# Cutting the first load of a row-normalising kernel into four row transfers

## The chip, the cores and the metric

The kernel runs on one core of one Trainium2 chip. The metric is the device time of one execution in microseconds (us). Most executions agree within 0.3%.

## The reference

```python
def setup_inputs():
    batch, dim = 1024, 4096
    return {"x": np.random.randn(batch, dim).astype(np.float32),
            "axis": -1, "eps": np.float32(1e-12)}

def reference(x, axis, eps):
    norm = np.sqrt(np.sum(x ** 2, axis=axis, keepdims=True) + eps)
    return (x / norm).astype(np.float32)
```

Each of 1024 rows of 4096 numbers is divided by its length. 16.78 MB are read and 16.78 MB are written.

## The kernel before

The input is cut into two tiles. A tile gives each of the 128 partitions R = 4 consecutive rows, 64 KB, so it holds 8.389 MB. Both loads are issued at the very start by SyncE, both stores later on the same queue.

```python
    R = 4
    ...
    x_t = x.rearrange("(p t r) d -> t p (r d)", t=n_tiles, r=R)
    out_t = out_flat.rearrange("(p t r) d -> t p (r d)", t=n_tiles, r=R)
    io = ctx.enter_context(tc.tile_pool(name="io", bufs=n_tiles))
    ...
    for i in range(n_tiles):
        g = RowGroups(nc, io, stats, scratch, D, R, eps_t)
        load = nc.sync.dma_start(out=g.flat(), in_=x_t[i])
        to_front(nc, load.ins)      # moves the load ahead of the opening barrier
        groups.append(g)

    for i, g in enumerate(groups):
        g.square_dve(R - 1)         # VectorE: sum of squares of row 3
        g.square_act(0)             # ScalarE: sum of squares of row 0
        g.norm(0)                   # square root (ScalarE), reciprocal (VectorE)
        g.scale(0)                  # VectorE
        g.square_act(1)
        g.norm(1)
        g.norm(R - 1)
        g.scale(1)
        g.scale(R - 1)
        g.square_act(2)
        g.norm(2)
        if i < n_tiles - 1:
            g.scale_by_both(2)      # 7/8 of the row on ScalarE, 1/8 on VectorE
        else:
            g.scale(2)
        store = nc.sync.dma_start(out=out_t[i], in_=g.flat())
```

The rows are scaled in place. Each tile has a buffer of its own, so no buffer is waited for.

Of the kernel before, what the change touches and what calls it, by code (L numbers as in the profile page):

```python
# [82 lines left out]
def to_front(nc, load):  # L83






    def move(program):  # L90
        blocks = program.main_func.blocks
        entry = blocks[0].instructions
        if any(i.name == load.name for i in entry):
            return
        body = next(
            b.instructions
            for b in blocks
            if any(i.name == load.name for i in b.instructions)
        )
        at = next(n for n, i in enumerate(body) if i.name == load.name)  # L100
        assert not body[at].sync_info.on_wait
        before = next(
            n
            for n, i in enumerate(entry)
            if i.engine == mybir.EngineType.SP and isinstance(i, mybir.InstDrain)
        )
        entry.insert(before, body.pop(at))

    nc.at_finalize(move)
# [72 lines left out]
@with_exitstack  # L182
def kernel(
    ctx: ExitStack,
    tc: tile.TileContext,
    x: bass.AP,
    axis: bass.AP,
    eps: bass.AP,
    out: bass.AP,
):  # L190
    nc = tc.nc
    P = nc.NUM_PARTITIONS

    assert isinstance(axis, int) and axis in (-1, len(x.shape) - 1)
    eps = float(eps)

    x = x.flatten_outer_dims()
    out_flat = out.flatten_outer_dims()
    N, D = x.shape
    R = 4  # L200
    assert N % (P * R) == 0
    n_tiles = N // (P * R)
# [4 lines that stand above are left out]
    scratch_pool = ctx.enter_context(tc.tile_pool(name="scratch", bufs=1))  # L207
    stats = ctx.enter_context(tc.tile_pool(name="stats", bufs=n_tiles))

    eps_t = scratch_pool.tile([P, 1], F32)  # L210
    nc.vector.memset(eps_t, eps)  # L211
    sq_act = scratch_pool.tile([P, D], F32)
    sq_dve = scratch_pool.tile([P, D], F32)
    scratch = {"act": sq_act, "dve": sq_dve}

    groups = []
    for i in range(n_tiles):
        g = RowGroups(nc, io, stats, scratch, D, R, eps_t)
        load = nc.sync.dma_start(out=g.flat(), in_=x_t[i])  # L219
        to_front(nc, load.ins)  # L220
        groups.append(g)

    for i, g in enumerate(groups):
        g.square_dve(R - 1)
        g.square_act(0)
        g.norm(0)
        g.scale(0)
# [8 lines that stand above are left out]
            g.scale_by_both(2)  # L236
# [3 lines that stand above are left out]
    gpsimd_waits_for_last_store(nc, store.ins)  # L240
# [35 lines left out]
```

## Time and profile before

| what | value |
|---|---|
| time, before the prediction | 81.85 us, median of 3 (81.83 to 81.91) |
| span of the profiled execution | 79.9 us |
| load 0 landed | 21.81 us |
| load 1 landed | 41.14 us |
| store 0, store 1 issued | 38.71 us, 56.50 us |
| VectorE, ScalarE busy | 26.7 us, 29.7 us |

A landing is read here from the start of the first instruction that waits for it. The profile has two more things: the page's share of the 16 DMA engines' time, and the packet records in the trace, which give start, duration and size of each packet that an engine moved. `prof` does not print them; they were read from the trace file. A record does not name its engine, so the records are taken in order of start, 16 at a time, one for each engine. In the steady state a packet of 64 KB has a record of 2.418 us, and the records of one engine follow each other every 2.414 us.

### The profile page before, as it was taken

What the parts mean: (1) busy time and instruction counts of PE and PEld (TensorE: products, weight loads), DVE (VectorE), ACT (ScalarE), POOL (GpSimd) and SP (SyncE); (2) the same over time, 40 slices, a digit from 0 to 9 for tenths busy, and PEclk for the clock granted to TensorE, in tenths of its full rate; (3) what the DMA queues carried; (4) which work ended last, traced back from release to release, by engine and by line L of the source; (5) the groups of instructions that cost most, each with busy time, mean ns of one, the idle gap of its engine ahead of it and who ended that gap; (6) DMA issues with size and microseconds to landing.
All of it is one profiled execution on the core that took longest, in us unless ns stands there. A gap on an engine that the chain in (4) does not pass through costs nothing.

```text
span 79.9 us, 93 instructions
## 1 busy us (share of the span) xinstructions
DVE 26.7 (33%) x21; ACT 29.7 (37%) x23; POOL 0.2 (0%) x4
## 2 busy tenths in 40 slices
DVE  0000000000099599960049995999200000000000
ACT  3200000000099999989349999950000000000000
POOL 1000000000000000000000000000000000000000
DMA  9099996599996699993899991999974999965990
GB/s 492 33 525 525 525 525 295 230 525 525 525 525 262 262 525 525 525 525 164 361 525 525 525 459 66 525 525 525 525 328 197 525 525 525 525 295 230 525 525 0
DMA packets 576, 33.55 MB, mean 420 GB/s; under 512 B 64, under 2 KB 64, under 8 KB 64
## 3 DMA queue, kind: packets, MB, share of 16 engines
q1 hardware_dynamic: 576, 33.55, 97.6%
HBM read 16.78 MB, written 16.78 MB: 420 GB/s over the span
## 4 chain that ended last, share of the span: by engine, by line
DMA 51%; ACT 10%; DVE 9%; SPq 0%; issue 0%
DMA xt<-in_x_dram 51%; ACT sq_act L33 9%; DVE xt L64 9%; ACT rstd L53 1%; SPq L219 0%; DVE rstd L59 0%
## 5 line engine op out<-in xcount | busy, mean ns | idle before, releaser
L33 ACT ACTIVATE sq_act<-xt 128x4096 f32<-128x4096 f32 x6 | 21.7, 3609 | 21.7 <-DMA xt<-in_x_dram 21.7
L42 DVE SCALAR_TENSOR_TENSOR sq_dve<-xt 128x4096 f32<-128x4096 f32 x2 | 8.8, 4424 | 25.7 <-DMA xt<-in_x_dram 25.7
L64 DVE TENSOR_SCALAR xt<-xt,rstd 128x4096 f32<-128x4096 f32 x7 | 16.5, 2353 | 0.2
L72 ACT ACTIVATE xt<-xt,rstd 128x3584 f32<-128x3584 f32 x1 | 3.3, 3282 | 0.2 <-DVE rstd L59 0.2
L53 ACT ACTIVATE rstd<-ssq,eps_t 128x1 f32<-128x1 f32 x8 | 2.1, 289 | 0.1
L59 DVE RECIPROCAL rstd<-rstd 128x1 f32<-128x1 f32 x8 | 1.3, 159 | 2.4 <-ACT rstd L53 2.4
L33 ACT ACT_TABLE_LOAD x1 | 1.3, 1283 | 1.3 <-PEq L257 1.3
L53 ACT ACT_TABLE_LOAD x1 | 1.3, 1283 | 0.0
L33 ACT ACTIVATION_READ_ACCUMULATOR sq_act<-xt 128x1 f32 x6 | 1.1, 186 | 0.0
L211 DVE MEMSET eps_t<- 128x1 f32 x1 | 0.1, 59 | 1.3 <-PEq L257 1.3
L78 DVE TENSOR_SCALAR xt<-xt,rstd 128x512 f32<-128x512 f32 x1 | 0.5, 486 | 0.0
L42 DVE DVE_READ_ACCUMULATOR sq_dve<-xt 128x1 f32 x2 | 0.2, 82 | 0.0
L257 POOL MEMSET const-bfloat16-1.0<- 128x1 bf16 x1 | 0.1, 103 | 0.0
L257 POOL MEMSET const-uint8-127<- 128x1 uint8 x1 | 0.1, 102 | 0.0
L257 POOL MEMSET const-float32-0.0<- 128x1 f32 x1 | 0.1, 100 | 0.2 <-issue 0.2
L257 POOL MEMSET const-float32-1.0<- 128x1 f32 x1 | 0.1, 99 | 0.0
## 6 DMA issues: line engine op xcount, KB each, us to landing
xt<-in_x_dram SPq DMA_DIRECT2D x2, 31.2
out_dram<-xt SPq DMA_DIRECT2D x2, 22.5
```

What stands on the lines that cost most here:

```text
L33: self.nc.scalar.activation(out=sq_a, in_=self.x[:, r], func=ACT_F.Square, accum_out=self.ssq[:, r : r + 1],)
L42: self.nc.vector.scalar_tensor_tensor(out=sq_v, in0=self.x[:, r], scalar=1.0, in1=self.x[:, r], op0=ALU.mult, op1=ALU.mult, accum_out=self ...
L53: self.nc.scalar.activation(out=self.rstd[:, r : r + n], in_=self.ssq[:, r : r + n], func=ACT_F.Sqrt, bias=self.eps_t,)
L59: self.nc.vector.reciprocal(out=self.rstd[:, r : r + n], in_=self.rstd[:, r : r + n])
L64: self.nc.vector.tensor_scalar_mul(out=self.x[:, r], in0=self.x[:, r], scalar1=self.rstd[:, r : r + 1])
L72: self.nc.scalar.activation(out=self.x[:, r, :cut], in_=self.x[:, r, :cut], func=ACT_F.Copy, scale=rstd,)
L78: self.nc.vector.tensor_scalar_mul(out=self.x[:, r, cut:], in0=self.x[:, r, cut:], scalar1=rstd)
L211: nc.vector.memset(eps_t, eps)
L257: nc = _bacc.Bacc("TRN2", target_bir_lowering=False, num_devices=1)
```

## The change

The intent: with tile 0 in four pieces, row 0 can be squared when a quarter of the tile is there, instead of both compute engines waiting until 21.8 us for all of it.

```diff
     for i in range(n_tiles):
         g = RowGroups(nc, io, stats, scratch, D, R, eps_t)
-        load = nc.sync.dma_start(out=g.flat(), in_=x_t[i])
-        to_front(nc, load.ins)
+        pieces = R if i == 0 else 1
+        for j in range(pieces):
+            part = slice(j * R * D // pieces, (j + 1) * R * D // pieces)
+            load = nc.sync.dma_start(out=g.flat()[:, part], in_=x_t[i][:, part])
+            to_front(nc, load.ins)
         groups.append(g)
```

## The prediction

> **What bounds the kernel now.** I began with the page of the profiled execution, because it says at once whether an engine or the transfers carry the span. These are lines of its parts 1, 2, 3 and 4:
>
> ```profile
> DVE 26.7 (33%) x21; ACT 29.7 (37%) x23; POOL 0.2 (0%) x4
> ...
> DMA packets 576, 33.55 MB, mean 420 GB/s; under 512 B 64, under 2 KB 64, under 8 KB 64
> ...
> q1 hardware_dynamic: 576, 33.55, 97.6%
> ...
> DMA 51%; ACT 10%; DVE 9%; SPq 0%; issue 0%
> ```
>
> The third line decides. The one queue moves 33.55 MB (16.78 MB of input, as much of output), and its packets fill 97.6% of the time of all 16 DMA engines. VectorE and ScalarE are busy for a third. The chain in the last line (51% transfer, then ScalarE and VectorE) is a trap: it adds up to 70%, because it stops at the issue of the last store, and that store is not on it. A chain of compute in it does not mean that compute is the bound.
>
> So I read the timeline next, for when the transfers are issued and when the compute engines are let go. Columns: start, duration, engine, line, operation, and idle time before it:
>
> ```profile
> 0.00 0.86 SPq L219 DMA_DIRECT2D xt<-in_x_dram  x2
> ...
> 21.81 3.62 ACT L33 ACTIVATE sq_act<-xt 128x4096 f32<-128x4096 f32 x1 [19.26 <-DMA xt<-in_x_dram]
> ...
> 38.71 18.13 SPq L239 DMA_DIRECT2D out_dram<-xt  x2
> 41.14 4.42 DVE L42 SCALAR_TENSOR_TENSOR sq_dve<-xt 128x4096 f32<-128x4096 f32 x1 [5.25 <-DMA xt<-in_x_dram]
> ...
> 54.12 2.35 DVE L64 TENSOR_SCALAR xt<-xt,rstd 128x4096 f32<-128x4096 f32 x1
> 56.50 0.34 SPq L239 DMA_DIRECT2D out_dram<-xt  x1
> ```
>
> Both loads are issued by 0.86 us. Load 0 has landed at 21.81 us and load 1 at 41.14 us, so one tile of 8.389 MB takes 41.14 - 21.81 = 19.33 us, 434 GB/s, and the start-up before the first tile is 21.81 - 19.33 = 2.48 us. Store 0 is issued at 38.71 us, 2.4 us before load 1 ends; store 1 at 56.50 us, while store 0 should end at about 41.14 + 19.33 = 60.5 us, so 4.0 us early. Neither store comes too late, hence the queue should never run dry. Two stretches, cut at those landings, confirm it (second column the length; last two the DMA share and GB/s):
>
> ```profile
> 21.80:41.14 19.34, 12.45 (x10) 16.55 (x12) 0.00 (x0) 1.00 1.00 434
> 41.14:60.00 18.86, 14.23 (x10) 11.87 (x10) 0.00 (x0) 1.00 0.99 431
> ```
>
> The DMA share is 1.00 during load 1 and 0.99 while store 0 runs. (Shares near the edges of a stretch are rounded by whole 64 KB packets.) My model of the kernel is then 2.48 us of start-up plus 4 x 19.33 = 77.32 us, 79.80 us, against a span of 79.9 us. The measured 81.85 us is 1.95 us more than the span; I carry that over unchanged.
>
> **What the Trainium skill says.** First, "Perfetto Trace Analysis", section DMA Optimizations: splitting transfers may let work start sooner and finish sooner "if DMA engines are generally idle". Here they are not: 97.6% busy. Second, "DMA: Bandwidth & Descriptors", Where 436 GB/s comes from: 16 ports x 32 B x 850 MHz = 435.2 GB/s. The trace agrees: 434 GB/s is 99.7% of it, so there is no faster rate for a different cutting to find. Third, the same page, Queues, rings and completion order: each DMA engine consumes the descriptors of a ring in order. The trace agrees where it can be seen: load 1, issued 0.4 us after load 0, lands one whole tile time after it. Fourth, the same page, Latency and other measured facts: copies of 16 KiB rows with a row pitch of 512 KiB in HBM ran at only 207 GB/s. The pitch here is 8 rows x 16 KiB = 128 KiB, before and after, and the trace shows 434 GB/s at it with 64 KiB runs; no trace yet shows it with 16 KiB runs.
>
> **The change part by part.** It removes one load of 128 x 64 KB, and adds four of 128 x 16 KB to the same bytes, on the same queue, still in front of load 1.
>
> *Issue.* Two loads took 0.86 us to issue, 0.43 each. Five take about 2.15 us, and load 1 is issued at about 1.7 us instead of 0.43. Load 0 keeps the queue full until about 21.8 us, so this is hidden. The first piece still covers 128 partitions, so all 16 engines start as before.
>
> *Packets.* A load has 128 packets of 64 KB, 8 per engine; now load 0 has 512 of 16 KB, 32 per engine, 24 more. The fixed cost of a packet is an estimate from the rate above: 64 KB takes 19.33 / 8 = 2.416 us on an engine, and at the skill's 27.2 B/ns (435.2 / 16) it would take 2.409; about 7 ns are left. So 24 x 7 = 0.17 us. The tile also gets three more completion writes per engine; their records in the trace last 9 ns each, 0.03 us. These 0.20 us lie on the saturated queue and so on the path that sets the end. It is probably an upper figure, as part of the 7 ns is the completion write of the tile; I take 0.15.
>
> *Compute of tile 0.* The pieces should land at about 2.48 + 4.87 n: 7.4, 12.2, 17.1 and 22.0 us. ScalarE squares rows 0, 1 and 2 as they land (3.6 us each); the order of the compiled program has VectorE now scale rows 0 and 1 and its eighth of row 2 before it squares row 3. After the last piece come VectorE's square 4.42, read-out 0.08, square root and reciprocal with their hand-overs about 0.5, and a scale of 2.35: 7.4 us. ScalarE's share of row 2 is done at about 17.1 + 3.6 + 0.2 + 0.3 + 0.4 + 3.3 = 24.9, sooner. So store 0 is issued at about 29.4 us instead of 38.71, 9.3 us earlier. It has nothing to gain from it: it stands in the queue behind load 1, which ends at 41.14 + 0.15 = 41.3 us. Gain on the end: 0.
>
> *Tile 1.* Its loads, order and operations are the same from the landing of load 1 on (both orders agree there), so store 1 is issued at about 56.6 us, still 4 us before store 0 ends.
>
> Sum: 81.85 + 0.15 = 82.00 us.
>
> **The rivals.** (a) *Earlier compute shortens the kernel.* For it: both compute engines idle some 20 us waiting for load 0, the longest waits of the kernel, and the chain names compute. Were the queue empty between load 1 and store 0, the 9.3 us would be worth something. Against it: a DMA share of 1.00 and 0.99 on either side of 41.14 us. At most a fraction of the 79.9 - 79.80 = 0.1 us that my model leaves over could come back: 81.75 us. (b) *16 KB packets cost much more than 7 ns.* Only one packet size is in this trace at rate, so the fixed cost is a difference of two near-equal numbers. At 30 ns, 24 more packets cost 0.7 us: 82.6 us. (c) *HBM dislikes 16 KB runs at a regular pitch.* If load 0 fell to 207 GB/s, it would take 40.5 us rather than 19.33, and the time would be about 103 us. Against it: consecutive runs on one engine were already spaced at 128 KB. I give it 3%. (d) *The start-up moves.* If descriptors of the first piece reach the engines sooner or later, the 2.48 us change by some tenths either way: 81.6 to 82.3 us. (e) *Store 1 is late* because tile 1's compute slips: it would need more than 4 us, and its operations are unchanged, so I give it 1%.
>
> **Range and chances.** The centre is 82.0. The runs of before spread by 0.08 us; start-up adds 0.2 either way, and the packet cost reaches up further than down, so 81.7 to 82.5 should hold it 8 times in 10. The 2% limits are 80.2 and 83.5 us. Faster would need a queue with 1.6 us to give, and it has about a tenth of a microsecond besides the start-up: 1%. Slower needs 70 ns per extra packet or rival (c): 4%. Within: 95%.
>
> **What would show it right or wrong.** In the changed profile, load 1 should be seen landed at 41.2 to 41.4 us (first square of tile 1), store 0 issued near 29.4 us and store 1 near 56.6 us, with the first square of tile 0 near 7.4 us. The packets rise from 576 by 384 data packets and 48 completion writes to 1008, the DMA share stays at 97% or more, and VectorE and ScalarE have the same busy time. If load 1 lands over 0.6 us later, the packet or pitch step is wrong; if it lands on time and the end is early, I missed an idle stretch of the queue; if row 3 of tile 0 is squared long before 22 us, the pieces do not run one behind the other.

## The result, and the profile after

The changed kernel takes 82.97 us (median of 4, 82.94 to 83.08); in the same rounds the kernel before takes 81.84 us (81.67 to 81.91). The ratio is 1.0139, 95% interval 1.0123 to 1.0155. The change costs 1.1 us; it is within 2%, but above the predicted range of 81.7 to 82.5 us.

The lines of the page of the changed kernel that answer to those shown of before (busy times of the engines, packets, the queue's share of the 16 DMA engines, the chain that ended last):

```profile
DVE 26.9 (33%) x21; ACT 29.9 (37%) x23; POOL 0.2 (0%) x4
...
DMA packets 1008, 33.55 MB, mean 414 GB/s; under 512 B 112, under 2 KB 112, under 8 KB 112
...
q1 hardware_dynamic: 1008, 33.55, 97.9%
...
DMA 50%; ACT 10%; DVE 9%; SPq 2%; issue 0%
```

The queue is as "full" as before, 97.9% against 97.6%, and the packets are the 1008 that were expected. Only the mean rate fell, from 420 to 414 GB/s. A busy share counts a packet that takes longer as busy, so it can't show a queue that has become slower.

The timeline of the changed kernel (start, duration, engine, line, operation, idle time before):

```profile
0.00 2.39 SPq L222 DMA_DIRECT2D xt<-in_x_dram  x5
...
7.31 3.62 ACT L33 ACTIVATE sq_act<-xt 128x4096 f32<-128x4096 f32 x1 [3.23 <-DMA xt<-in_x_dram]
...
21.98 4.43 DVE L42 SCALAR_TENSOR_TENSOR sq_dve<-xt 128x4096 f32<-128x4096 f32 x1 [0.16 <-DMA xt<-in_x_dram]
...
29.40 28.61 SPq L242 DMA_DIRECT2D out_dram<-xt  x2
...
42.31 4.43 DVE L42 SCALAR_TENSOR_TENSOR sq_dve<-xt 128x4096 f32<-128x4096 f32 x1 [12.98 <-DMA xt<-in_x_dram]
```

Down to the store everything is where the prediction put it: first square at 7.31 us, last piece there at 21.98 us, store 0 issued at 29.40 us. The loss is between the landings of the two loads, 42.31 - 21.98 = 20.33 us where it was 19.33. Two stretches of the changed kernel, load 1 and store 0 (second column the length, last two the DMA share and GB/s):

```profile
22.00:42.29 20.29, 6.93 (x4) 2.91 (x2) 0.00 (x0) 1.00 1.01 413
...
42.29:61.60 19.31, 14.23 (x10) 11.87 (x10) 0.00 (x0) 1.00 1.00 434
```

Load 1 runs at 413 GB/s at a DMA share of 1.01; store 0 at 434, as before. Load 1 itself was not changed. The packet records show where it slowed. The table gives the mean record of the 16 engines for the last packets of load 1 and the first of store 0:

| packet on each engine | before, us | changed, us (least to most) |
|---|---|---|
| last but one of load 1 | 2.418 | 2.419 |
| last of load 1 | 2.427 | 3.497 (3.018 to 3.821) |
| first of store 0 | 2.418 | 2.418 |

So the last packet of load 1 is stretched on every engine, by 1.07 us on average; behind the start-up no other packet is. The account of the landing of load 1: 42.31 - 41.14 = 1.17 us later, of which 21.98 - 21.81 = 0.17 us come from load 0 in pieces and 1.00 us from this stretch. The span grew from 79.9 to 81.1 us.

### The profile page after: what moved, and what is told of

The parts are those of the page before. It is cut to its first block, busy times and chain, and to the rows that moved or that the text cites. A ratio compares the mean times of both kernels' runs of the same rounds, so it can differ in the third digit from the quotient of the medians. Undisturbed runs are those within 1.5% of the kernel's fastest.

```text
span 81.1 us, 102 instructions
## 1 busy us (share of the span) xinstructions
DVE 26.9 (33%) x21; ACT 29.9 (37%) x23; POOL 0.2 (0%) x4
## 2 busy tenths in 40 slices
DMA packets 1008, 33.55 MB, mean 414 GB/s; under 512 B 112, under 2 KB 112, under 8 KB 112
## 3 DMA queue, kind: packets, MB, share of 16 engines
q1 hardware_dynamic: 1008, 33.55, 97.9%
## 4 chain that ended last, share of the span: by engine, by line
DMA 50%; ACT 10%; DVE 9%; SPq 2%; issue 0%
DMA xt<-in_x_dram 50%; ACT sq_act L33 9%; DVE xt L64 9%; SPq L222 2%; ACT rstd L53 1%; DVE rstd L59 0%
```

## The experiments

**The theory, T1.** The store is issued 9.3 us earlier than before, and stands in the queue long before load 1 ends. A store that is queued so early stretches the last packets of the load ahead of it. **The rival, T2.** The stretch comes from the pieces themselves, for instance from the number of transfers or descriptors that passed through the queue before. In a kernel that is otherwise as changed, delaying the store tells them apart; so does an early store in a kernel without pieces.

### Pieces, with the store as late as before (e1_pieces_late)

```diff
+    def idle_pass(self, r, width):
+        self.nc.vector.tensor_scalar_mul(
+            out=self.scratch["dve"][:, :width], in0=self.x[:, r, :width],
+            scalar1=self.rstd[:, r : r + 1])
...
         g.scale(1)
+        if i == 0:
+            for width in (4096, 4096, 4096, 4096):
+                g.idle_pass(R - 1, width)
         g.scale(R - 1)
```

> Four pieces kept; four extra VectorE passes (2.35 us each, into the scratch tile) hold store 0 back from 29.4 to about 38.8 us, as late as in the kernel before. Theory T1 (a store that stands in the queue well before the end of load 1 stretches the last load packets; it is the earliness of the store that costs): the last packets of load 1 take 2.42-2.43 us again, load 1 lands at about 41.3 us, time 82.0 us (only the packet cost of 0.17 is left). Rival T2 (the stretch comes from the pieces themselves, for instance from the number of descriptors or transfers that went through the rings before): last packets 3.0 to 3.8 us as in the changed kernel, load 1 lands at 42.3, time 83.0 us.

Measured: 81.94 us (81.72 to 82.19), before 81.82 us, ratio 1.0028 (1.0007 to 1.0050). The last packet of load 1 takes 2.420 us on average, 2.426 at most. The timeline of this run around the store:

```profile
38.75 0.35 SPq L252 DMA_DIRECT2D out_dram<-xt  x1
...
41.11 4.42 DVE L42 SCALAR_TENSOR_TENSOR sq_dve<-xt 128x4096 f32<-128x4096 f32 x1 [2.43 <-DMA xt<-in_x_dram]
```

With the store back at 38.75 us, load 1 lands at 41.11 us. Four useless passes of VectorE made the kernel a microsecond faster. T2 falls: the pieces are all still there.

### One whole load, with an early store (e2_whole_early)

```diff
-        g.square_act(2)
-        g.norm(2)
-        if i < n_tiles - 1:
-            g.scale_by_both(2)
-        else:
-            g.scale(2)
+        if i > 0:
+            g.square_act(2)
+            g.norm(2)
+            g.scale(2)
```

> One whole load as before; row 2 of tile 0 is left unscaled (wrong result on purpose for those rows), so that store 0 is issued at about 34.7 us instead of 38.7. T1: the last packets of load 1 take 3.0 to 3.8 us although nothing was cut into pieces, load 1 lands near 42.2 us, time 82.8 to 82.9 us. T2: last packets 2.42 us, load 1 lands at 41.14, time 81.85 us.

Measured: 83.05 us (82.64 to 83.27), before 81.82 us, ratio 1.0148 (1.0115 to 1.0180). The result is wrong on purpose in the rows left unscaled. The last packet of load 1 takes 3.646 us (3.426 to 4.072). Its timeline:

```profile
34.61 0.35 SPq L237 DMA_DIRECT2D out_dram<-xt  x1
...
42.49 4.42 DVE L42 SCALAR_TENSOR_TENSOR sq_dve<-xt 128x4096 f32<-128x4096 f32 x1 [7.91 <-DMA xt<-in_x_dram]
```

This kernel does less work than the kernel before, has no pieces, and is 1.2 us slower: load 1 lands at 42.49 us. With both runs, T1 is shown: the time of the store's issue decides.

One more rival has to go. In the changed kernel and in e2, VectorE and ScalarE also stand idle at the end of load 1 (from 29.4 and 34.6 us), so their idleness could be the cause. The end of load 0 settles it: both engines are idle there in the kernel before, and its last packets take 2.419 us; both are idle there in e8_turns (below), where a 2 MB store is queued behind load 0, and they take 3.590 us. In e5_both_pieces (below) the stretch is there although ScalarE squares from 36.62 to 40.14 us.

### How early is too early (e3_pieces_mid, e4_pieces_near)

The same edit as in e1, with other widths:

```diff
-            for width in (4096, 4096, 4096, 4096):
+            for width in (4096, 4096):                  # e3_pieces_mid
+            for width in (4096, 4096, 4096, 2048):      # e4_pieces_near
```

> Four pieces, two extra VectorE passes: store 0 issued at about 34.1 us, some 4 us before the last packets of load 1 start. T1, if the cost depends only on the store being queued before the last load packet starts: the same stretch of about 1.05 us per engine, time 83.0. If instead the cost grows with how long the store waits: about half, 82.5. T2: 83.0 with the stretch.

> Four pieces, three and a half extra VectorE passes: store 0 issued at about 37.6 us, shortly before the last packets of load 1 start (37.9 to 38.4), its descriptors about 1 us later (the first load packet started 1.0 us after its issue). T1 with the descriptors' arrival as what counts: no stretch, 82.0 us. T1 with the issue as what counts: stretch, 83.0. T2: 83.0.

Measured, one run each (state unknown): 82.78 us and 82.40 us. The cost by the time of issue, with the runs above:

| kernel | store 0 issued, us | last packet of load 1, mean us | stretch over 2.418 |
|---|---|---|---|
| changed | 29.40 | 3.497 | 1.08 |
| e3_pieces_mid | 34.19 | 3.345 | 0.93 |
| e2_whole_early | 34.61 | 3.646 | 1.23 |
| e4_pieces_near | 37.88 | 2.756 | 0.34 |
| before | 38.71 | 2.427 | 0.01 |
| e1_pieces_late | 38.75 | 2.420 | 0.00 |

How long the store waits hardly matters between 29.4 and 34.6 us (0.93 to 1.23 us, in no order). The two clean expectations for e4, all or nothing, both missed: at 37.88 us a third of the stretch is left, and 0.83 us later, in the kernel before, nothing. The last packets of load 1 start at about 38 us, so the kernel before issues its store just in time to be spared. Nothing in its source says so.

### Where in the load it lies, and whether packet sizes matter (e5_both_pieces, e6_store_rows)

```diff
-        pieces = R if i == 0 else 1
+        pieces = R                                      # e5_both_pieces
```

```diff
-        store = nc.sync.dma_start(out=out_t[i], in_=g.flat())
+        pieces = R if i == 0 else 1                     # e6_store_rows
+        for j in range(pieces):
+            part = slice(j * R * D // pieces, (j + 1) * R * D // pieces)
+            store = nc.sync.dma_start(out=out_t[i][:, part], in_=g.flat()[:, part])
```

> Load 1 is cut into four pieces too, so the last load packets are 16 KB (0.61 us each) and store 0 is early (29.4 us). If the stretch is a wait at the turn from load to store (T1, turn), it stays about 1.0 us and all of it lies in the last one or two 16 KB packets of each engine (1.4 to 1.7 us instead of 0.61); time about 83.1 us. If it is a slower last stretch of data (for example the store's reads sharing the engine with the last 64 KB of load), it scales with the packet or spreads over the last four packets: a stretch of 0.25 us in all with the last packet, or 0.25 us in each of four; the first gives 82.3 us.

> Loads as in the changed kernel; store 0 is cut into four row stores of 16 KB packets, queued from about 15 to 29.4 us. If what is read ahead of the first store packet (64 KB or 16 KB) sets the wait, the last packet of load 1 is stretched by about a quarter of 1.05 us, time 82.4 us with 0.2 us for the smaller store packets. If the wait belongs to the turn whatever the packet of the store is, the stretch stays near 1.05 us, time 83.2 us.

Measured: e5 83.04 us (before 81.90, ratio 1.0137, 1.0112 to 1.0161); e6 83.22 us (before 81.90, ratio 1.0160, 1.0139 to 1.0181). They were run on another chip. In e6 the first row of the store is queued at 15.28 us, and the last packet of load 1 takes 3.466 us: whether the store's packets have 16 or 64 KB doesn't matter, nor does another 14 us of waiting. In e5 the last load packets of 16 KB take, in order and on average, 0.616, 0.872, 1.210, 0.711 us, and the very last 0.611 on 15 of the 16 records counted with it (the sixteenth is the first of the store). So the stretch is again about 1 us whatever the load's packet, but it isn't at the turn, as I had expected: it lies in the third and fourth packets from the end, two packets or so before the engine's write side reaches the store, and the very last load packet runs at full speed. The lengthened records lie between 38.2 and 41.5 us; load 1 had landed at 42.5 us.

The Trainium skill's page "DMA: Bandwidth & Descriptors", section Two DMAs through the same engine are not ordered, says that descriptors of a queue start in order but are pipelined, and that an engine's read and write sides are separate queues. A read side that reaches the store ahead of the write side would fit this place, and would fit that a store issued 2.4 us before the landing costs nothing. This is argued; the records don't show the two sides apart.

### Whether every turn costs (e7_act_queue, e8_turns, e12_three_turns)

A turn is a place where an engine passes from packets of a load to packets of a store, or back.

```diff
-        store = nc.sync.dma_start(out=out_t[i], in_=g.flat())
+        queue = nc.scalar if i == 0 else nc.sync        # e7_act_queue, on the changed kernel
+        store = queue.dma_start(out=out_t[i], in_=g.flat())
```

```diff
+    nc.vector.memset(sq_dve, 0.0)                       # e8_turns, on the kernel before
...
+        if i == 1:
+            nc.sync.dma_start(out=out_t[1][:, :D], in_=sq_dve)
         load = nc.sync.dma_start(out=g.flat(), in_=x_t[i])
-        to_front(nc, load.ins)
+        if i == 0:
+            to_front(nc, load.ins)
```

```diff
+    zeros = scratch_pool.tile([P, D], F32)              # e12_three_turns, on the kernel before
+    nc.vector.memset(zeros, 0.0)
...
-        load = nc.sync.dma_start(out=g.flat(), in_=x_t[i])
-        to_front(nc, load.ins)
+        pieces = 1 if i == 0 else R
+        for j in range(pieces):
+            part = slice(j * R * D // pieces, (j + 1) * R * D // pieces)
+            if i == 1 and j % 2 == 0:
+                nc.sync.dma_start(out=out_t[1][:, part], in_=zeros)
+            load = nc.sync.dma_start(out=g.flat()[:, part], in_=x_t[i][:, part])
+            if i == 0:
+                to_front(nc, load.ins)
```

> Store 0 is issued at about 29.4 us from ScalarE, on another queue, so that it runs interleaved with the rest of load 1 (about 5 packets per engine left) instead of behind it. If each turn between load and store costs (T1, turn), many packets in the stretch from 30 to 55 us are longer than 2.42 us per packet moved, and the DMA moves clearly less than 434 GB/s there. If the cost is only where a queue passes from a load transfer to a store transfer, the rate stays at 434 GB/s. In both cases load 1 lands late, at 53 us or more, store 1 is issued at 68 us or more, the queue runs dry before it and the time is about 90 us.

> One-piece loads; between load 0 and load 1 a store of 2 MB of zeros from the scratch tile is queued early (about 5 us), into rows that store 1 overwrites later. Three turns: load 0 to store, store to load 1, load 1 to store 0. T1: the last packets of load 0 are stretched by about 1.1 us; the turn from store to load tells whether the other direction costs: if the cost is of any turn, about 1 us there too, if only of load to store, under 0.1 us. Store 0 would be issued at 42 to 45 us with load 1 ending at 47 to 48, early enough for a stretch there as well. Time about 81.85 + 4.85 for the store + 1.1 to 3.3 us for the turns = 87.8 to 90 us.

> Queue order: load 0 in one piece, 2 MB of zeros out, half of load 1, 2 MB of zeros out, the other half of load 1, store 0; everything queued well ahead. If every passage from load to store on the queue costs alike, three stretches of about 1.1 us per engine; if the first costs and later ones less (1.17 and then 0.37 in the run with two turns), about 1.1, then 0.4 or less, then 0.4 or less. Passages from store to load under 0.05 us. Time about 81.85 + 2 x 4.9 + 1.1 + 0 to 2.2 = 92.7 to 95 us.

Measured, one run each (state unknown): e7 90.41 us, e8 88.71 us, e12 93.07 us. All three give the right result.

In e7 the store of tile 0 mixes with load 1. Two stretches of that run, around the first store packets and the mixed part after them:

```profile
31.30:35.00 3.70, 0.00 (x0) 0.00 (x0) 0.00 (x0) 1.00 0.66 283
35.00:52.00 17.00, 0.00 (x0) 0.00 (x0) 0.00 (x0) 1.00 1.00 432
```

The load packets that run when the store comes in take 3.730 us on average, 1.31 more than usual. After that the engines take a packet of each queue in turn for 14 us, and all records but two (2.455 and 2.653 us, at the first turn) stay at about 2.418 us. (The first line counts a packet by where it starts or ends, so its 283 GB/s is coarse; the 432 GB/s over 17 us is not.) So, after the first, the turns between load and store cost nothing in this run. The 90 us come from elsewhere: load 1, sharing the engines, lands at 52.23 us, store 1 can only be issued at 67.64 us, and store 0 had landed about 6 us before that.

In e8 and e12 the turns come one after another on one queue, all queued ahead of the turn:

| turn, load to store | e8_turns: stretch of the load packet | e12_three_turns |
|---|---|---|
| first | 1.17 us (record of 3.590) | 1.17 us (3.584) |
| second | 0.36 us (2.783) | none (0.611 where 0.611 is usual) |
| third | - | none (0.611 to 0.619) |

In these runs the packets of the store after the first turn keep 0.611 us, and the turn back from store to load shows at most 0.02 us on average. In these three runs, one execution each, the full price is thus paid once, at the first store of the execution that is queued behind loads. The 0.36 us of the second turn in e8 have no counterpart in e12, and I have no cause for them. One difference: the store of that turn was issued at 41.45 us, 2.45 us before the last packets of load 1 started, whereas the second and third stores of e12 were queued by 7.1 and 43.2 us, at least 5.7 us before the last 64 KB of the load ahead of them started on an engine.

### Whether a small store takes the price off (e9_warm_other, e10_warm_same, e11_small_turn)

```diff
+    small = scratch_pool.tile([P, 128], F32)            # on the changed kernel
+    nc.vector.memset(small, 0.0)
+    nc.scalar.dma_start(out=out_t[1][:, :128], in_=small)   # e9_warm_other; out_t[0] in e10_warm_same
     groups = []
```

```diff
+    zeros = scratch_pool.tile([P, 128], F32)            # e11_small_turn, on the kernel before
+    nc.vector.memset(zeros, 0.0)
...
+        if i == 1:
+            nc.sync.dma_start(out=out_t[1][:, :128], in_=zeros)
         load = nc.sync.dma_start(out=g.flat(), in_=x_t[i])
-        to_front(nc, load.ins)
+        if i == 0:
+            to_front(nc, load.ins)
```

> The changed kernel plus one small store of zeros (128 x 512 B), issued at about 3 us from ScalarE's queue, into rows that store 1 overwrites later. Theory T1-first (the cost belongs to the first store of the execution only, when load packets are already queued around it, as the first of many turns in the run on two queues suggests): a stretch of about 1.1 us per engine appears in the 16 KB packets of load 0 at about 4 to 7 us, and the last packets of load 1 are stretched by at most 0.4 us; time 83.0 to 83.4 us because the cost has only moved. If the small store hides its cost in the start-up, 82.0 to 82.4 us. Rival T1-turn (each first passage of a queue from load to store costs, whatever was stored before): the last packets of load 1 are again stretched by 1.05 us; time 83 us with nothing at 4 to 7 us, or 84 us with both.

> As the run before it, but the small store goes to the rows that store 0 writes. If the first touch of an address range is what costs, the stretch at the end of load 1 is gone here (below 0.05 us) and of the order of 0.4 us or more in the other; if it is the first store of any address, the two are the same within 0.1 us per engine.

> One-piece loads; a store of zeros of only 64 KB in all (512 B to a partition) is queued on the same queue between load 0 and load 1, some 17 us before load 0 ends. If the stretch belongs to the passage of a queue from load to store, whatever is stored, the last packets of load 0 are stretched by about 1.1 us as with the 2 MB store, time about 83 us. If it needs a store of some length behind the load (data of the store read ahead), the stretch of load 0 is under 0.3 us and the time 81.9 to 82.3 us. Store 0 stays late relative to load 1, so no stretch at the end of load 1 in either case.

Measured: e9 83.08 us (before 81.82, ratio 1.0154, 1.0138 to 1.0170); e10 83.28 us (before 81.82, ratio 1.0176, 1.0159 to 1.0194); e11 81.93 us, one run (state unknown), beside 81.82. In e9 and e10 the last packet of load 1 takes 3.358 and 3.302 us, so the stretch is still there, 0.94 and 0.88 us, and the small store caused none where it ran. In e11 a store of 64 KB in all is queued behind load 0 from 1.1 us on, and the last packets of load 0 take 2.426 us: a short store causes no stretch at all, and store 0, issued 2.6 us before load 1 landed, causes none either. So "the first store of the execution" was too simple: 64 KB neither trigger the stretch nor take it away; 2 MB trigger it and, in e12, leave nothing for the later turns. That the first touch of the output's addresses is the cause is unlikely, as e10 had touched the rows that store 0 begins with; it isn't ruled out for every address in them.

No version beat the kernel before. It already avoids the stretch, and its queue runs at 434 GB/s from the first landing to the end.

## Why the prediction was wrong

What held, by its own steps:

- **The bound.** The queue sets the time. e2 did less compute and was slower, because load 1 landed later; e1 did more and was not.
- **Issue.** Five loads took 2.39 us (2.15 said), hidden. The opening table load of ScalarE moved from 1.26 to 2.80 us with it, which cost nothing.
- **Packets.** Load 0 in pieces landed 0.17 us later; 0.15 was said. The landing alone is a weak witness: in e1's profile the same pieces had landed by 21.77 us, 0.04 us before the whole load, so start-up differs by about as much from run to run. With the store held late (e1), the ratio is 1.0028, 0.23 us; the medians differ by 0.12 us. The size rests best on the records: the 16 KB packets' records follow each other every 0.607 us, 4 x 0.607 = 2.428 against 2.414 us for 64 KB, so some 5 ns for each packet more, about 0.11 us for the 24, and three more completion writes of 9 ns an engine.
- **Rival (c), the row pitch.** The pieces ran at full rate (16 KB every 0.607 us on each of 16 engines, 432 GB/s) at their pitch of 128 KiB. The slow rate that the Trainium skill ("DMA: Bandwidth & Descriptors", Latency and other measured facts) gives for a pitch of 512 KiB was not tried; no run here shows it.
- **Compute of tile 0, and tile 1.** The first square at 7.31 us against 7.4, the early store at 29.40 us against "about 29.4", and tile 1's unchanged 15.35 us from landing to store (57.66 - 42.31; before 56.50 - 41.14 = 15.36) are as said.

What failed is one sentence of the step on tile 0: "It has nothing to gain from it: it stands in the queue behind load 1 ... Gain on the end: 0." The earlier issue was taken as neutral because the store stands behind load 1. It isn't neutral. The early store stretched the last packet of load 1 by 1.07 us on the average engine, 1.00 us on the landing, and with it everything after: shown by taking the early store out of the changed kernel (e1) and putting it into the kernel without pieces (e2). The sum that should have stood is 81.85 + 0.17 + 1.00 = 83.02 us; 82.97 was measured. No rival named it: they ask what the pieces do to the loads, or whether the early store gains anything, and none asks what the early store does to a load already in the queue. That the time stayed within 2%, which was given 95%, was luck in this respect: no term of the sum held the loss that moved it.

The list of signs was also too narrow. It said that load 1 landing over 0.6 us late means that the packet or pitch step is wrong. Load 1 landed 1.17 us late with both right. The sign should have been taken packet by packet.

What stays open is the mechanism inside the DMA engine: why a long store queued early slows the last stretch of the load for about 1 us, why it does so in full once only, and what the second turn of e8 paid for.

## What to carry to other kernels

On this saturated queue, issuing a transfer earlier was not free although it couldn't start earlier: ask what it does to the transfer ahead of it. Here it was best for the first large store to join the queue during the last packet time of the loads; whether another kernel has the same stretch, its packet records must show. When a busy share doesn't move and the time does, compare the records of single packets: a stretched packet counts as busy. A tuned kernel can owe a microsecond to an accident of timing, which a change elsewhere takes away.

## What the Trainium skill lacked or had wrong

- "DMA: Bandwidth & Descriptors" (Queues, rings and completion order; Rules for kernel authors): nothing there says that a store queued behind a load can slow that load. The runs show stretches of 0.88 to 1.31 us a DMA engine at the first long store (8.389 MB or 2 MB) of every run that queued it early behind the loads or beside them, 0.34 in e4 where it came almost late enough, none when the store was issued 2.4 us before the landing.
- The same page's rule on overlapping transfers with compute, in the table of rules, advises to issue a DMA early. For the first store here this lost 1.0 us against a store issued 9.35 us later (e1); the rule has no exception for it.
- "Perfetto Trace Analysis", DMA Optimizations: that chunks "may allow some to start sooner" held (the first square, which waits for the first piece, started at 7.31 instead of 21.81 us). Its condition of idle DMA engines for a sooner end was right to be heeded: the engines were 97.6% busy, and nothing was gained. The page doesn't warn that what starts sooner can lose time downstream, 1.1 us here.
- "DMA: Bandwidth & Descriptors", Where 436 GB/s comes from: the ceiling of 435 GB/s is confirmed; 434 GB/s was reached by load and store, 432 by a mix of both. The same section says that for transfers between HBM and SBUF the HBM side, about 358 GB/s, binds; in these runs of one core it did not.
